# A tuned decoder layer whose opening takes sixteen column chunks instead of twelve, in four block groups instead of five

## The chip, the cores and the metric

One core of a Trainium2 chip runs the whole layer. The metric is the device time of one execution in microseconds, the median of several runs. Of the five engines this text speaks of PE (TensorE: matrix products), DVE (VectorE), ACT (ScalarE) and SP (SyncE, which here only issues DMAs, strictly in the order in which the program lists them).

## The reference

A decoder layer on 256 tokens of width 2048, all in float32. The part that the change touches is the first feed-forward block with its modulation:

```python
c_act = jax.nn.silu(c)
mod = (c_act @ w_ada[l] + b_ada[l]).reshape(b, N_MOD, D_MODEL)       # 9 vectors of 2048
h = modulate(rms_norm(x, norm_ffn1[l]), mod[:, 0], mod[:, 1])        # h * (1 + scale) + shift
x = x + 0.5 * mod[:, 2][:, None, :] * swiglu(h, w_ffn1_gu[l], w_ffn1_down[l])
...
gate, up = jnp.split(h @ w_gu, 2, axis=-1)                           # each 5632 wide
return (jax.nn.silu(gate) * up) @ w_down
```

After it come a retention and a window-attention mixer with their projections, a second feed-forward block and a last norm.

## The kernel before

**Products.** A float32 product is made of three products of rounded halves. A weight block is 128 x 512. ACT rounds it to its high part (`wh`, L350), DVE subtracts to get the low part (`wl`, L352), and PE multiplies, for each of the two halves of the 256 tokens, high by high, low activation by high weight, and high by low weight (L342, L343, L344): six products of 512 columns a block. Blocks are mostly handled in pairs (one ACT cast, one DVE subtraction of 128 x 1024, twelve products). `wsp` holds three such pairs, so casts and subtractions run at most a little ahead of PE. Weights come by DMA into `raw`, four buffers of 1 MB.

**Conditioning.** Each of the nine vectors of `mod` has 16 parts of 128 values, and each part needs one row block of `w_ada` (1 MB, called a row here), multiplied and summed on DVE by `ada_pass` (L206): two passes of 1024 columns a row in the opening, four of 512 later.

**The opening.** The activation `h` needs shift and scale (vectors 0 and 1), that is 32 rows, before all of it is there. So that PE need not wait for all of them, the contraction over 16 blocks is cut into groups (`bounds`), and `group(ks)` makes the rows and then the columns `h` of the next group while PE multiplies those of the present one. In each group PE visits all column chunks in turn (512 columns of the gate or the up half; an even and an odd chunk make a pair that gives 512 columns of the result). `visit` loads the chunk's blocks of that group into `raw` and multiplies; the sums are kept in `part` between groups (`to_parts`: copied by ACT the first time, L984, added by DVE later, L982). `stay` leaves the last two chunks of a group in PSUM, since the next group visits the chunks in the opposite order and starts with them. In the last group `swiglu_up` adds both parts (L665, L666), applies silu on ACT and multiplies (L669), and the result is turned by four PE transposes a tile (L477). A ring of two rows (`ring`, the halves of `tiles[0]`) holds the rows of the opening.

Before the change there are twelve chunks (`EARLY = 6` pairs) and groups of 2, 3, 3, 4 and 4 blocks. Pairs 6 to 10 are then made by `ffn_up`, whole contraction at once; pairs 6 to 9 are turned by DMA transposes (`turn_by_dma`: two ACT copies, a transpose issued by SP, two ACT copies), pair 10 by PE.

**Later rows.** The next three vectors (48 rows) are made by `conditioning`, a generator paced by `tick`: each half of a weight load of `ffn_up` and of the down projection advances it by `rate` quarter rows. It starts after the opening, at 192 quarter rows for 150 halves, from a ring of two rows in a slot of its own.

**What sets the order.** SP follows the program. The order on PE, DVE and ACT is made by a scheduler when the program is built; on the chip each engine follows that order and waits where an operand is not there.

Of the kernel before, what the change touches and what calls it, by code (L numbers as in the profile page):

```python
# [9 lines left out]
F32 = mybir.dt.float32  # L10
# [7 lines left out]
P = 128  # L18
# [3 lines left out]
NT = S // P  # L22
# [3 lines left out]
KB = 4  # L26
EPS = 1e-6
RAWS = 4
EARLY = 6

RH, RDK, RDV = 8, 128, 256
QH, KVH, HD = 32, 8, 64
# [45 lines left out]
def layer_kernel(  # L78
# [40 lines left out]
    def nm(s):  # L119
        uid[0] += 1  # L120
        return f"{s}_{uid[0]}"
# [110 lines left out]
    def two_rows():  # L232

        both = slot()
        turn = [both[:, :D], both[:, D:]]

        def place():
            turn.append(turn.pop(0))
            return turn[-1]

        return place

    def conditioning(outputs, place, ahead, behind):


        tiles = [(m, k) for m, _, _ in outputs for k in range(KD)]
        held = {}
        step = 0
        for m, gain, row in outputs:
            sums = ada_sums()  # L250
            for k in range(KD):
                for q in range(AQ):
                    for i in range(step // AQ, min((step + ahead) // AQ + 1, len(tiles))):
                        if i not in held:
                            held[i] = place()
                            ada_load(*tiles[i], held[i])
                    if behind is not None and step < 2 * AQ:
                        with tc.issue_after(behind.ins):
                            ada_pass(k, held[step // AQ], sums, q)
                    else:  # L260
                        ada_pass(k, held[step // AQ], sums, q)
                    step += 1
                    if k == KD - 1 and q == AQ - 1:
                        ada_end(m, slice(0, KD), sums, gain)
                        if row is not None:
                            gate_out(m, row)
                    yield
# [19 lines left out]

    def set_pace(outputs, halves, place, ahead):
        assert next(pace["steps"], None) is None
        pace["steps"] = conditioning(outputs, place, ahead, pace["behind"])  # L290
        pace["rate"] = len(outputs) * KD * AQ / halves
        pace["due"] = 0.0

    def tick():
        pace["due"] += pace["rate"]
        while pace["due"] >= 1.0:
            pace["due"] -= 1.0
            next(pace["steps"], None)
# [47 lines left out]
    def split(pool, tag, src, n, hi_engine="act"):  # L346
        k = src.shape[1]
        hi = pool.tile([P, 2, n], F32R, tag=tag + "h", name=nm(tag + "h"))[:, :k, :]
        lo = pool.tile([P, 2, n], F32R, tag=tag + "l", name=nm(tag + "l"))[:, :k, :]
        cast.append(nc.scalar.copy(hi, src).ins)  # L350
        del cast[:-1]
        nc.vector.tensor_sub(lo, src, hi.bitcast(F32))  # L352
        return hi, lo
# [3 lines left out]
    def pair_tile():  # L357
        return asp.tile([P, 2, CH], F32, tag="a", name=nm("a"))
# [525 lines left out]
    tiles = [slot(), part[0]]  # L884
    ring = [tiles[0][:, :D], tiles[0][:, D:]]

    def part_of(n):
        at = (n % 4) * NT * CH
        return [part[n // 4][:, at + t * CH : at + (t + 1) * CH] for t in range(NT)]

    early = [ada_sums() for _ in range(2)]

# [21 lines left out]
    def group(ks):  # L914

        for k in ks:
            for m in (1, 0):
                if (m, k) not in rows_of:
                    place(m, k)
                for q in range(passes):  # L920
                    ada_pass(k, rows_of[m, k], early[m], q, passes)
                if ks[0] == 0:
                    ada_end(m, slice(k, k + 1), early[m], 0 if m else None, passes)
                yield
        if ks[0] > 0:
            for m in (1, 0):
                ada_end(m, slice(ks[0], ks[-1] + 1), early[m], 0 if m else None, passes)
        for k in ks:
            ps = bank()
            for t in range(NT):  # L930
                xn = t512()[:, :P]
                nc.scalar.mul(xn, x_sb[:, t, k * P : (k + 1) * P], r[t])
                nc.tensor.transpose(ps[:, t * P : (t + 1) * P], xn, ident)
            modulated(held, k, ps[:, :S], 0, act=True)
# [7 lines left out]
    r = [Root(ssq, t).all() for t in range(NT)]  # L942
    for t in range(NT):
        nc.vector.tensor_scalar(out=r[t], in0=r[t], scalar1=HALF, scalar2=None, op0=ALU.mult)
    bounds = (0, 2, 5, 8, 12, 16)
    groups = [range(a, b) for a, b in zip(bounds, bounds[1:])]


# [3 lines left out]
    def load_blocks(n, ks):  # L952
        raw = raws.tile([P, KB, CH], F32, tag="raw", name=nm("raw"))
        c0 = (n % 2) * DFF + (n // 2) * CH
        nc.sync.dma_start(
            raw[:, : len(ks), :],
            gu[ks[0] * P : (ks[-1] + 1) * P, c0 : c0 + CH].rearrange("(k p) n -> p k n", p=P),
        )
        return raw

    def visit(n, ks, raw, ends, step=2):
        starts = n not in banks
        if starts:
            banks[n] = [acc_bank() for _ in range(NT)]
        for a in range(0, len(ks), step):
            b = min(a + step, len(ks))
            hl = slice(ks[a], ks[a] + b - a)
            wh, wl = split(wsp, "w", raw[:, a:b, :], CH)
            products(
                banks[n],  # L970
                held.hi[:, hl, :],
                held.lo[:, hl, :],
                wh,
                wl,
                starts and a == 0,
                b == len(ks) and ends,
            )

    def to_parts(n):
        for p, b in zip(part_of(n), banks.pop(n)):  # L980
# [3 lines left out]
                nc.scalar.copy(p, b)  # L984
        moved.add(n)

    for _ in group(groups[0]):
        pass
    for g, ks in enumerate(groups):
        final = g == len(groups) - 1  # L990
        order = chunks if g % 2 == 0 else chunks[::-1]
        coming = iter(()) if final else group(groups[g + 1])
        due = 0 if final else 2 * len(groups[g + 1])
        stay = () if final else order[-2:]
        for i, n in enumerate(order):
            visit(n, ks, load_blocks(n, ks), n not in stay)
            last = len(order) - 2
            for _ in range((i + 1) * due // last - i * due // last if i < last else i == last):
                next(coming, None)
            if n in stay:  # L1000
                continue
            if not final:
                to_parts(n)
            elif n % 2:
                swiglu_up(
                    banks.pop(n - 1), banks.pop(n), tiles, n // 2, (part_of(n - 1), part_of(n))
                )
    gate = gate_row()
    tiles.append(slot())
    place = two_rows()  # L1010
    set_pace([(2, None, 0.5), (4, 1, None), (3, None, None)], 150, place, AQ)
    ffn_up(held, gu, tiles, EARLY, turned=range(EARLY, DFF // CH - 1))
    gate_in = gate_load(gate, 2)
    wi = w_in[0]
# [395 lines left out]
```

## Time and profile before

| | |
|---|---|
| runs shown | 2403.92, 2406.2, 2407.77 us; median 2406.2 |
| the profiled execution | 2404.94 us, of which 2403.2 us are the span from its first to its last instruction |
| PE busy | 2369.4 us, 99% of the span |
| DVE, ACT busy | 1693.1 us (70%), 1300.2 us (54%) |
| HBM read | 595.06 MB, 248 GB/s over the span |

A product's record shows its latency, so records of PE overlap: how fast PE works is read from the distance between the starts of products that follow each other, and lost time from the idle rows and from distances that are longer.

### The profile page before, as it was taken

To read this page: it belongs to the slowest core of one execution; us is meant where nothing else is said; L and a number is where in the kernel's file an instruction comes from. 1 tells how busy PE (TensorE), PEld (TensorE's weight loads), DVE (VectorE), ACT (ScalarE), POOL (GpSimd) and SP (SyncE) were. 2 spreads that over 40 slices of the span, in tenths; PEclk is the share of its full clock that TensorE was granted. 3 is DMA by queue.
4 is the path that set the end of the run, shared out by engine and by line. 5 is a ranking of instruction groups with operands and counts; after the bars stand their busy time and mean duration, and the time that the engine had idled before them with its cause. 6 is when DMAs were issued, how large, how long until landed. Compare 5 with 4: busy or idle time off the path is not lost. (4 is left out here: it accounts for less than half of the span.)

```text
span 2403.2 us, 28875 instructions
## 1 busy us (share of the span) xinstructions
PE 2369.4 (99%) x10662; PEld 1936.5 (81%) x10662; DVE 1693.1 (70%) x2720; ACT 1300.2 (54%) x1811; POOL 5.6 (0%) x14
## 2 busy tenths in 40 slices
PE   7999999999999999999999999999999999999998
PEld 4778888888788887778888888887888888888886
DVE  6998787778877667886766766768655555545656
ACT  6544545454546566765555554456445445454544
POOL 0000000000000000000000000000000000000000
PEclk9999999999999999999999999999999999999999
DMA  9987688998876797766679787765677777765563
GB/s 347 338 334 285 230 308 301 379 320 304 302 269 228 243 286 219 232 229 210 217 256 289 263 282 264 280 198 200 225 239 237 248 256 240 261 219 189 183 205 126
DMA packets 309550, 615.31 MB, mean 256 GB/s; under 512 B 75105, under 2 KB 75489, under 8 KB 290593
## 3 DMA queue, kind: packets, MB, share of 16 engines
q1 hardware_dynamic: 307906, 606.82, 74.1%
q0 software_dynamic: 928, 5.61, 0.6%
q8 instruction: 83, 1.36, 0.2%
q10 hardware_dynamic: 576, 1.05, 0.1%
q14 instruction: 57, 0.47, 0.1%
HBM read 595.06 MB, written 2.12 MB: 248 GB/s over the span
## 5 line engine op out<-in xcount | busy, mean ns | idle before, releaser
L352 DVE TENSOR_TENSOR wl<-raw,wh 128x1024 fp32r<-128x1024 f32 (+1 forms) x806 | 967.9, 1206 | 559.4 <-ACT wh L350 554.6
L350 ACT CAST wh<-raw 128x1024 fp32r<-128x1024 f32 (+1 forms) x806 | 836.9, 1041 | 938.6 <-PE pa L343 921.7
L342 PE MATMUL pa<-wh,hh 128*128 128x512 f32 x2192 | 857.1, 392 | 2.2 <-ACT wh L350 1.7
L343 PE MATMUL pa<-wh,hl 128*128 128x512 f32 x2192 | 856.2, 391 | 1.6 <-DVE hl L599 1.6
L344 PE MATMUL pa<-wl,hh 128*128 128x512 f32 x2192 | 784.2, 392 | 2.4 <-DVE wl L352 2.2
L342 PEld LDWEIGHTS pa<-wh,hh 128*128 128x128 f32 x2192 | 412.0, 188 | 90.1 <-issue 2.8
L343 PEld LDWEIGHTS pa<-wh,hl 128*128 128x128 f32 x2192 | 412.1, 188 | 89.7 <-issue 3.0
L344 PEld LDWEIGHTS pa<-wl,hh 128*128 128x128 f32 x2192 | 409.4, 188 | 92.9 <-DVE wl L352 6.8
L343 PE MATMUL pa<-wh,a 128*128 128x512 f32 x944 | 365.3, 389 | 0.1
L342 PE MATMUL pa<-wh,a 128*128 128x512 f32 x944 | 349.8, 390 | 1.0 <-ACT wh L350 0.5
L344 PE MATMUL pa<-wl,a 128*128 128x512 f32 x944 | 349.0, 390 | 1.4 <-DVE wl L352 1.4
L344 PEld LDWEIGHTS pa<-wl,a 128*128 128x128 f32 x944 | 176.9, 188 | 39.9 <-DVE wl L352 3.2
L342 PEld LDWEIGHTS pa<-wh,a 128*128 128x128 f32 x944 | 177.1, 188 | 39.7 <-DVE slot L1292 1.0
L343 PEld LDWEIGHTS pa<-wh,a 128*128 128x128 f32 x944 | 177.1, 188 | 37.2 <-DVE a L385 0.5
L206 DVE CUSTOM_DVE_ANT_0 slot<-slot,cact 128x512 f32<-128x512 f32 (+1 forms) x252 | 192.6, 812 | 14.4 <-DMA slot<-in_w_ada_dram 14.3
L206 DVE CUSTOM_DVE_ANT_0 raw<-raw,cact 128x512 f32<-128x512 f32 (+1 forms) x260 | 167.0, 695 | 46.0 <-DMA raw<-in_w_ada_dram 39.1
L510 ACT COPY slot<-back 128x512 uint16<-128x512 uint16 x124 | 82.7, 766 | 0.0
L385 DVE TENSOR_TENSOR a<-slot,a 128x512 fp32r<-128x512 f32 x118 | 80.6, 683 | 1.7 <-ACT a L384 1.7
L384 ACT CAST a<-slot 128x512 fp32r<-128x512 f32 x118 | 72.7, 617 | 0.0
L494 ACT COPY flat<-t 128x512 uint16<-128x512 uint16 x112 | 63.5, 616 | 9.6 <-DVE t L1197 9.2
L206 DVE DVE_READ_ACCUMULATOR2_ANT sums<- 128x1 f32 x512 | 41.8, 82 | 0.0
L982 DVE TENSOR_TENSOR slot<-slot,pa 128x512 f32<-128x512 f32 x56 | 35.7, 677 | 0.0
(197 smaller groups left out, 1163.9 us busy)
## 6 DMA issues: line engine op xcount, KB each, us to landing
raw<-in_w_ffn_gu_dram SPq DMA_DIRECT2D x152, 1024.0 KB, 5.2
raw<-in_w_in_dram SPq DMA_DIRECT2D x104, 1024.0 KB, 5.4
raw<-in_w_ffn_down_dram SPq DMA_DIRECT2D x88, 1024.0 KB, 5.1
slot<-in_w_ada_dram SPq DMA_DIRECT2D x76, 1024.0 KB, 7.4
raw<-in_w_ada_dram SPq DMA_DIRECT2D x64, 1024.0 KB, 5.0
raw<-in_w_ffn_gu_dram SPq DMA_DIRECT2D x24, 768.0 KB, 6.9
raw<-in_w_swa_branch_dram SPq DMA_DIRECT2D x16, 1024.0 KB, 5.1
raw<-in_w_ret_branch_dram SPq DMA_DIRECT2D x16, 1024.0 KB, 5.3
```

The lines of the kernel that those rows point to most:

```text
L206: nc.vector.tensor_tensor_reduce(out=w[:, at], in0=w[:, at], in1=cact[:, at], scale=1.0, scalar=0.0, op0=ALU.mult, op1=ALU.add, accum_out= ...
L342: nc.tensor.matmul(ps, ah[:, j, ts], wh[:, j, :], start=first, stop=False)
L343: nc.tensor.matmul(ps, al[:, j, ts], wh[:, j, :], start=False, stop=False)
L344: nc.tensor.matmul(ps, ah[:, j, ts], wl[:, j, :], start=False, stop=last)
L350: cast.append(nc.scalar.copy(hi, src).ins)
L352: nc.vector.tensor_sub(lo, src, hi.bitcast(F32))
L384: nc.scalar.copy(hi, v)
L385: nc.vector.tensor_sub(lo, v, hi.bitcast(F32))
L494: nc.scalar.copy(planes[:, i, :], words(src)[:, :, i])
L510: nc.scalar.copy(into[:, :, :, i], held["turned"][:, i])
L982: nc.vector.tensor_add(p, p, b)
```

## The change

`EARLY` becomes 8, so the opening takes 16 column chunks, and `bounds` becomes (0, 2, 6, 12, 16): groups of 2, 4, 6 and 4. `visit` now loads its blocks itself, in pieces of at most four blocks: a visit of the group of six takes two `raw` buffers. The sums of chunks 0 and 1 are kept in four tiles of the `back` pool, those of 14 and 15 in two `pair_tile`s, since `part` holds twelve. The visiting order is such that the last group runs forward. Beside the last group eight of the later 48 rows are made (one quarter row a pair of blocks); these take their place in `raw`, among the weights, until the slot of the two-row ring is free. The remaining 160 quarter rows follow at 160 to 117 halves. Of the eight pairs of the opening, pairs 1 and 5 are turned by DMA, the other six by PE; pairs 6 and 7, turned by DMA before, are now turned by PE.

```diff
-EARLY = 6
+EARLY = 8
...
-    def conditioning(outputs, place, ahead, behind):
+    def conditioning(outputs, place, behind):
...
-                    for i in range(step // AQ, min((step + ahead) // AQ + 1, len(tiles))):
+                    for i in range(step // AQ, min((step + pace["ahead"]) // AQ + 1, len(tiles))):
...
+    beside = [pair_tile() for _ in range(2)]
+    behind = [[back.tile([P, CH], F32, tag="back", name=nm("back")) for _ in range(NT)] for _ in range(2)]
...
     def part_of(n):
-        at = (n % 4) * NT * CH
-        return [part[n // 4][:, at + t * CH : at + (t + 1) * CH] for t in range(NT)]
+        if n < 2:
+            return behind[n]
+        if n >= 14:
+            return [beside[n - 14][:, t, :] for t in range(NT)]
+        at = ((n - 2) % 4) * NT * CH
+        return [part[(n - 2) // 4][:, at + t * CH : at + (t + 1) * CH] for t in range(NT)]
...
-    bounds = (0, 2, 5, 8, 12, 16)
+    bounds = (0, 2, 6, 12, 16)
...
-    def visit(n, ks, raw, ends, step=2):
+    def visit(n, ks, ends, ticks=False):
...
+        raw_of = [(load_blocks(n, part), part) for part in (ks[:KB], ks[KB:]) if part]
+        pieces = [
+            (raw[:, a : a + 2, :], part[a : a + 2])
+            for raw, part in raw_of
+            for a in range(0, len(part), 2)
+        ]
...
+            if ticks:
+                tick()
...
+    ROWS_FFN1 = [(2, None, 0.5), (4, 1, None), (3, None, None)]
+    row_ring = []
+
+    def place_row():
+        return row_ring[0]() if row_ring else raw_row()
...
-        order = chunks if g % 2 == 0 else chunks[::-1]
+        if final:
+            set_pace(ROWS_FFN1, 32 * 192 // 32, place_row, 1)
+        order = chunks if (len(groups) - g) % 2 else chunks[::-1]
...
-            visit(n, ks, load_blocks(n, ks), n not in stay)
+            visit(n, ks, n not in stay, final)
+            if final:
+                turn_step()
...
-                    banks.pop(n - 1), banks.pop(n), tiles, n // 2, (part_of(n - 1), part_of(n))
+                    banks.pop(n - 1),
+                    banks.pop(n),
+                    tiles,
+                    n // 2,
+                    (part_of(n - 1), part_of(n)),
+                    n // 2 in (1, 5),
...
-    place = two_rows()
-    set_pace([(2, None, 0.5), (4, 1, None), (3, None, None)], 150, place, AQ)
+    row_ring.append(two_rows())
+    pace["rate"] = (192 - 32) / 117
+    pace["ahead"] = AQ
```

The first place where the order differs is DVE in the third group. Before (groups of three blocks), two visits stand there: `wl` is a weight's low part, `slot_129` with `cact` a row's pass, `slot_127` with `pa` the addition of a kept sum.

```order
L352 TENSOR_TENSOR wl_1226<-raw_1221,wh_1225 128x1024
L206 ISA slot_129,sums_131<-slot_129,cact 128x1024
L206 ISA sums_131 128x1
L206 ISA slot_129,sums_131<-slot_129,cact 128x1024
L206 ISA sums_131 128x1
L352 TENSOR_TENSOR wl_1242<-raw_1221,wh_1241 128x512
L982 TENSOR_TENSOR slot_127<-slot_127,pa_1188 128x512
L982 TENSOR_TENSOR slot_127<-slot_127,pa_1189 128x512
L352 TENSOR_TENSOR wl_1261<-raw_1256,wh_1260 128x1024
```

After, the third group has six blocks a visit, and the same names read:

```order
L998 TENSOR_TENSOR slot_127<-slot_127,pa_1713 128x512
L998 TENSOR_TENSOR slot_127<-slot_127,pa_1714 128x512
L206 ISA slot_129,sums_137<-slot_129,cact 128x1024
L206 ISA sums_137 128x1
L206 ISA slot_129,sums_137<-slot_129,cact 128x1024
L206 ISA sums_137 128x1
L353 TENSOR_TENSOR wl_1811<-raw_1776,wh_1810 128x1024
L353 TENSOR_TENSOR wl_1835<-raw_1830,wh_1834 128x1024
L353 TENSOR_TENSOR wl_1851<-raw_1830,wh_1850 128x1024
L998 TENSOR_TENSOR slot_127<-slot_127,pa_1772 128x512
```

Between one chunk's two additions and the next chunk's there are now three full subtractions where there were one and a half.

The second place is SP in the last group. Before, there are only weight loads (L955), until the opening ends and the first row of the ring follows:

```order
L955 DMA raw_2364<-in_w_ffn_gu_dram 128x4x512
L955 DMA raw_2422<-in_w_ffn_gu_dram 128x4x512
L955 DMA raw_2458<-in_w_ffn_gu_dram 128x4x512
L327 DMA raw_2521<-in_w_ffn_gu_dram 128x4x512
L201 DMA slot_2518<-in_w_ada_dram 128x2048 x2
```

After, a row (L201, into a `raw` buffer) follows every second weight load (L963):

```order
L963 DMA raw_2434<-in_w_ffn_gu_dram 128x4x512
L963 DMA raw_2472<-in_w_ffn_gu_dram 128x4x512
L201 DMA raw_2507<-in_w_ada_dram 128x2048
L963 DMA raw_2522<-in_w_ffn_gu_dram 128x4x512
L963 DMA raw_2560<-in_w_ffn_gu_dram 128x4x512
L201 DMA raw_2595<-in_w_ada_dram 128x2048
```

The third place is DVE at the row `raw_2507` of that list. Its four passes stand between the two subtractions of one weight load, where before (L352) nothing but additions (L666) and products (L669) of the finished pair stood:

```order
L352 TENSOR_TENSOR wl_2255<-raw_2234,wh_2254 128x1024
L666 TENSOR_TENSOR slot_127<-pa_2178,slot_127 128x512
L666 TENSOR_TENSOR slot_127<-pa_2179,slot_127 128x512
L669 TENSOR_TENSOR t_2212<-t_2212,slot_127 128x512
L352 TENSOR_TENSOR wl_2275<-raw_2270,wh_2274 128x1024
```

After:

```order
L353 TENSOR_TENSOR wl_2437<-raw_2434,wh_2436 128x1024
L206 ISA raw_2507,sums_2351<-raw_2507,cact 128x512
L206 ISA sums_2351 128x1
L206 ISA raw_2507,sums_2351<-raw_2507,cact 128x512
L206 ISA sums_2351 128x1
L206 ISA raw_2507,sums_2351<-raw_2507,cact 128x512
L206 ISA sums_2351 128x1
L206 ISA raw_2507,sums_2351<-raw_2507,cact 128x512
L206 ISA sums_2351 128x1
L353 TENSOR_TENSOR wl_2454<-raw_2434,wh_2453 128x1024
```

The weight `wl_2454` behind the four passes is thus queued behind the landing of the row.

More of the change, by code (lines that the diff above doesn't have):

```diff
@@ L289, in set_pace @@
         assert next(pace["steps"], None) is None
-        pace["steps"] = conditioning(outputs, place, ahead, pace["behind"])
+        pace["steps"] = conditioning(outputs, place, pace["behind"])
         pace["rate"] = len(outputs) * KD * AQ / halves
         pace["due"] = 0.0
+        pace["ahead"] = ahead
     def tick():
@@ L964, in visit @@
             banks[n] = [acc_bank() for _ in range(NT)]
[L965 to L968, printed above, removed]
+        raw_of = [(load_blocks(n, part), part) for part in (ks[:KB], ks[KB:]) if part]
[4 more added lines that the diff above has]
+        ]
+        for raw, part in pieces:
+            a, b = part[0] - ks[0], part[-1] + 1 - ks[0]
+            hl = slice(part[0], part[-1] + 1)
+            wh, wl = split(wsp, "w", raw[:, : len(part), :], CH)
             products(
```

## The prediction

> **What bounds the kernel now.** I read the page's engine shares first, then a table of stretches, then what PE waited for, then DVE's own order.
>
> ```profile
> PE 2369.4 (99%) x10662; PEld 1936.5 (81%) x10662; DVE 1693.1 (70%) x2720; ACT 1300.2 (54%) x1811; POOL 5.6 (0%) x14
> ```
>
> PE is busy for 99% of the span, so only its idle time and its slow stretches can be won. The table of stretches shows where they lie. Its columns are the stretch in us, its length, busy time and records of PE, PEld, DVE, ACT and POOL, granted clock, DMA share, GB/s. The bounds are the starts of the first product of each block group (counted off: 144, 216, 216, 288 and 288 products).
>
> ```profile
> 0.00:25.96 25.96, 9.83 (x15) 3.76 (x15) 13.19 (x47) 13.67 (x32) 0.20 (x4) 1.00 0.87 319
> 25.96:64.10 38.14, 37.13 (x148) 29.23 (x149) 31.46 (x46) 27.30 (x46) 0.00 (x0) 1.00 0.97 369
> 64.10:114.23 50.13, 49.94 (x224) 40.90 (x222) 45.68 (x72) 25.04 (x37) 0.00 (x0) 1.00 0.89 334
> 114.23:171.30 57.07, 52.95 (x226) 40.09 (x225) 54.11 (x88) 25.88 (x41) 0.00 (x0) 1.00 0.88 326
> 171.30:238.04 66.74, 66.74 (x300) 54.82 (x299) 60.22 (x85) 32.12 (x45) 0.00 (x0) 1.00 0.82 304
> 238.04:308.18 70.14, 70.14 (x331) 58.26 (x330) 56.23 (x83) 39.82 (x51) 0.00 (x0) 1.00 0.65 230
> 308.18:720.00 411.82, 410.58 (x1813) 337.93 (x1812) 324.09 (x575) 203.97 (x241) 2.23 (x4) 1.00 0.88 314
> 720.00:2403.20 1683.20, 1672.04 (x7617) 1371.48 (x7615) 1108.16 (x1730) 932.42 (x1324) 3.17 (x6) 1.00 0.70 233
> ```
>
> PE idles 16.1 us before the first product, which the change does not touch: the first group still has two blocks and the same first loads. Of the rest of the opening, the third group stands out: PE idles 4.1 us in it and DVE is busy for 54.11 of 57.07 us. PE's waits up to 500 us name the releaser (total, times, longest):
>
> ```profile
> ...
> PE pa L344 <- DVE wl L352: 2.2, 5, 0.8
> PE pa L342 <- ACT wh L350: 1.7, 2, 0.9
> PE pa L343 <- DVE hl L599: 1.6, 2, 1.2
> PE pa L342 <- DVE slot L982: 0.5, 1, 0.5
> ```
>
> All but the ACT row are DVE being late.
>
> **Prices.** From PE's timeline (start, duration): two of the first products, a pair of transposes, and two products with 50 others between them. Below them the group of PE's transposes of results (count, busy us, mean ns).
>
> ```profile
> 29.12 0.63 PE L342 MATMUL pa<-wh,hh 128*128 128x512 f32 x1
> 29.55 0.63 PE L343 MATMUL pa<-wh,hl 128*128 128x512 f32 x1
> ...
> 118.04 0.38 PE L933 MATMUL ps<-small_c,t 128*128 128x128 f32 x2
> ...
> 128.06 0.39 PE L342 MATMUL pa<-wh,hh 128*128 128x512 f32 x1
> ...
> 139.66 0.39 PE L343 MATMUL pa<-wh,hl 128*128 128x512 f32 x1
> ```
>
> ```profile
> L477 PE MATMUL ps<-small_c,t 128*128 128x128 f32 x32 | 4.5, 272 | 0.0
> ```
>
> A product costs (139.66 - 128.06)/51 = 0.2275 us, so a pair of blocks 2.73. One transpose's record is 0.27 long and that of two 0.38, so the second starts 0.11 after the first: 0.11 each. The first products stand 0.43 apart although the granted clock reads 1.00; that slow start, some 2.9 us in all until 32 us, stays.
>
> DVE's starts in a stretch without idle time:
>
> ```profile
> 94.92 1.22 DVE L352 TENSOR_TENSOR wl<-raw,wh 128x1024 fp32r<-128x1024 f32 x1
> 96.05 1.21 DVE L206 CUSTOM_DVE_ANT_0 slot<-slot,cact 128x1024 f32<-128x1024 f32 x1
> ...
> 97.20 1.22 DVE L206 CUSTOM_DVE_ANT_0 slot<-slot,cact 128x1024 f32<-128x1024 f32 x1
> ...
> 98.34 0.68 DVE L352 TENSOR_TENSOR wl<-raw,wh 128x512 fp32r<-128x512 f32 x1
> 98.95 1.27 DVE L982 TENSOR_TENSOR slot<-slot,pa 128x512 f32<-128x512 f32 x2
> 100.14 1.22 DVE L352 TENSOR_TENSOR wl<-raw,wh 128x1024 fp32r<-128x1024 f32 x1
> ...
> 115.62 0.42 DVE L599 TENSOR_TENSOR hl<-t,hh 128x256 fp32r<-128x256 f32 x1
> ...
> 293.48 0.69 DVE L206 CUSTOM_DVE_ANT_0 slot<-slot,cact 128x512 f32<-128x512 f32 x1
> ...
> 294.10 0.68 DVE L206 CUSTOM_DVE_ANT_0 slot<-slot,cact 128x512 f32<-128x512 f32 x1
> ```
>
> From start to start: a subtraction of a pair 1.14, of one block 0.61; a row of two passes 2.29; an addition 0.60; a column of `h` 0.42 at most; a pass of 512 0.61.
>
> **The group sizes.** DVE's work against PE's, group by group. Before, third group: 12 visits of 1.75 for subtractions is 21.0, 8 rows 18.3, 20 additions 12.0, 4 columns 1.7: 53.0 us, against 216 products and 8 transposes, 50.0 us. DVE is overloaded by 6%, and the stage takes 57.07. The second comes to 45.7 of 49.8, the fourth to 59.4 of 66.4. After, the same sums:
> - first group: 16 x 1.14 + 8 x 2.29 + 4 x 0.42 = 38.2 us of DVE against 192 products, 43.7 us (87%; before 28.7 of 32.8, also 87%);
> - second: 32 x 1.14 + 12 x 2.29 + 24 x 0.60 + 6 x 0.42 = 80.9 against 384 products and 12 transposes, 88.7 (91%);
> - third: 48 x 1.14 + 8 x 2.29 + 28 x 0.60 + 4 x 0.42 = 91.5 against 576 products, 131.9 with transposes (69%);
> - last: 32 x 1.14 + 32 passes at 0.61 + 48 additions and multiplications = 84.8 against 384 products and 48 transposes, 92.6 (92%; before 53.9 of 70.8).
>
> So no group overloads DVE any more, because the same 32 rows are spread over a third more products. What DMA must bring falls too. For the old third group it is 36 blocks (0.262 MB) and 8 rows (1.049 MB), 17.8 MB in 49.1 us of products, 363 GB/s; the new third needs 256, the second 336, the last 272. The first group needs 16.8 MB in 43.7 us, 384 GB/s, and before it was 12.6 MB in 32.8, the same.
>
> **What PE loses after.** Before, from 25.96 to 308.18 PE took 282.2 us for 1152 products (262.1), 28 transposes of `h` (3.1) and 48 of results (5.3): 11.7 lost, of which about 7.1 in the third group, 2.9 in the slow start and 1.8 elsewhere in the first; the other stages come out at nothing in sum. After I charge: the slow start 2.9; the first group 1.9, since most of its 1.8 is one wait on ACT at its end (0.9 us, with some slow restarts), and I take that to come once a group, not once a visit; the second group 0.4, as its DVE share is that of the old second and fourth, which lost 0.3 each; the third 0.2; the last 0.6. Sum 6.0, so 5.7 us are won. A bound on each: nothing lost beyond the slow start would win 8.8; the old third group's loss once more in the new second would make it a loss of 1.0.
>
> In the first group a rule weighs against the change. The last row here has DMA's highest sustained rate in the opening:
>
> ```profile
> 60.00:80.00 20.00, 20.00 (x92) 16.43 (x91) 16.15 (x24) 13.28 (x25) 0.00 (x0) 1.00 1.02 388
> ```
>
> At the first stage's 369 GB/s the new first group is 1.8 us short of PE's pace, the old one 1.3; the four loads in flight cover that. The Trainium skill, "DMA: Bandwidth & Descriptors", section Specifications, gives about 358 GB/s as the limit of HBM for one core: by it the new group would be 3.2 us short, the old 2.3, and I would take 0.4 us off the gain. The 388 above goes past that figure, so I leave the sum as it is.
>
> **The eight rows beside the last group.** A row now sits in `raw`, and DVE's order puts its four passes between two subtractions, which wait behind it. The trace has such rows in later stages. The first line is DVE's waits for them between 850 and 1500 us, the second a stretch of that stage, the last the page's DMA issues (count, size, median us to landing):
>
> ```profile
> ...
> DVE raw L206 <- DMA raw<-in_w_ada_dram: 29.6, 23, 3.2
> ...
> ```
>
> ```profile
> 1000.00:1500.00 500.00, 499.31 (x2317) 408.07 (x2316) 353.02 (x658) 285.25 (x434) 0.00 (x0) 1.00 0.74 248
> ```
>
> ```profile
> ...
> slot<-in_w_ada_dram SPq DMA_DIRECT2D x76, 1024.0 KB, 7.4
> raw<-in_w_ada_dram SPq DMA_DIRECT2D x64, 1024.0 KB, 5.0
> ```
>
> Each wait is 1.3 us, and PE lost 0.7 us in 500 there. But DVE is 71% busy there, not 92%. Eight rows at 1.3 us make 10.4 us of waiting; DVE's slack in the last group is 92.6 - 84.8 = 7.8, and it runs up to one pair, 2.7 us, ahead: 10.5. So the waits just fit, and 0.6 us is what I charge; with none 0, with 3.2 us each 25.6 - 10.5 = 15.1. In the order three subtractions, each paced by PE at 2.73, mostly lie between the freeing of a row's buffer and its first pass, 8.2 us against a landing of 5.0 to 7.4: nearer to the low end.
>
> **The rest.** Pairs 1 and 5 go to DMA and 6 and 7 come from it: 16 PE transposes fewer and 16 more, zero. Their ACT copies lie beside an ACT that is 57% busy in the last group (39.82 of 70.14). SP passes four transposes in the last group; their planes are copied by ACT a visit earlier, so the loads behind them do not wait. After the opening 160 quarter rows come at 1.37 a half, not 1.28: 0.09 x 0.61 = 0.05 us of DVE on 2.73. The fullest stretch there leaves room:
>
> ```profile
> 660.00:680.00 20.00, 20.00 (x90) 16.53 (x90) 17.84 (x35) 9.66 (x12) 0.00 (x0) 1.00 0.97 352
> ```
>
> 17.84 would become 18.2 of 20: nothing, or at worst the 1.2 us that PE now idles from 308 to 720 once more. Everything after 720 keeps its order.
>
> **Sum.** The profiled execution took 2404.94 us, 1.3 below the median of 2406.2. Less 5.7 it is 2399.2; against the median, 2400.5.
>
> **Rivals.** First, the waits come back at the group borders. In the old third group four waits (1.15, 0.42, 0.52, 0.40 us by the waits, 3.2 with the restarts) came in its first 13 us, when `h` was late because a row's pass had waited for DMA:
>
> ```profile
> 109.78 0.68 DVE L352 TENSOR_TENSOR wl<-raw,wh 128x512 fp32r<-128x512 f32 x1
> 112.19 1.23 DVE L206 CUSTOM_DVE_ANT_0 slot<-slot,cact 128x1024 f32<-128x1024 f32 x1 [1.72 <-DMA slot<-in_w_ada_dram]
> ```
>
> The other borders cost next to nothing. One such border leaves a gain of 2.5 (2403.7), two a small loss of 0.7 (2406.9). For it: two borders of the new order, at 91% and 87% of DVE. Against: in the new order the rows ahead of them have longer leads.
>
> Second, and slower: the rows in `raw` hold up DVE in the last group. At 3.2 us each PE loses 15.1 there instead of 0.6: 2400.5 + 14.5 = 2415.0. It decides the sign from waits of about 2.1 us a row (16.8 - 10.5 = 6.3 lost, which eats the gain).
>
> Third, the later stage does not take 1.37 quarter rows a half: 152 halves with 192 quarter rows become 120 with 160, and if DVE's 0.05 us a half were not hidden at all PE would lose 120 x 0.05 = 6 us, 2406.5. Against it stands the free tenth of DVE above.
>
> **Chances.** About 0.2%, 4.8 us, is what a measurement of this kernel can tell from no change. My forecast gets 0.68, of which 0.62 lie over that bound (the sum is 0.9 above it, its best case 4.0) and 0.06 under it. The first rival gets 0.16 and the third 0.03, all within the bound; the second 0.13, slower. That is faster 0.62, same 0.25, slower 0.13. The range reaches from 8.8 won on the profiled execution (2396.1, and half a us for the spread of runs) to two bad borders at 2406.9; outside it lies the second rival.
>
> **What would show it.** The last products of the four groups should end near 75, 164, 296 and 389 us, the last against 308.2 plus 384 products, 395.6, for the same work before. DVE should be busy for 65 to 75% of the third group, and `PE pa L344 <- DVE wl` should nearly vanish from the waits before 300. If PE idles over 3 us in the last group behind a subtraction whose predecessor on DVE is a row's pass that waited for DMA, the second rival holds; if it idles at about 75 or 164 behind `hl`, the first.

## The result, and the profile after

The changed kernel takes 2401.06 us (median of 13 runs, 2398.03 to 2402.71), the kernel before 2404.52 beside it (13 runs, 2403.4 to 2411.71): a ratio of 0.998, 95% interval 0.9971 to 0.9988. That is 0.1 to 0.3% faster, 3.5 us between the medians. The profiled execution took 2398.28 us, its span 2396.5.

The page's engine shares hardly differ from before:

```profile
PE 2365.2 (99%) x10662; PEld 1937.3 (81%) x10662; DVE 1696.6 (71%) x2707; ACT 1302.2 (54%) x1807; POOL 5.6 (0%) x14
```

The stretches of the changed kernel, cut at the first product of each of its four groups (192, 384, 576 and 384 products), with the columns as in the prediction:

```profile
24.77:74.36 49.59, 47.40 (x196) 37.43 (x197) 41.44 (x58) 35.81 (x58) 0.00 (x0) 1.00 0.99 376
74.36:162.50 88.14, 88.14 (x394) 72.68 (x392) 80.70 (x113) 40.56 (x50) 0.00 (x0) 1.00 0.92 340
162.50:296.48 133.98, 133.44 (x593) 109.36 (x592) 100.53 (x132) 61.62 (x82) 0.00 (x0) 1.00 0.75 260
296.48:388.16 91.68, 91.68 (x426) 76.15 (x425) 86.42 (x151) 55.50 (x72) 0.00 (x0) 1.00 0.88 299
388.16:720.00 331.84, 330.07 (x1462) 272.39 (x1461) 270.99 (x486) 167.34 (x200) 2.23 (x4) 1.00 0.90 318
```

The group that lost most is gone. In the old third group DVE was busy for 54.11 us beside 50.0 of PE's own work. Now it is busy for less than PE's work in every group: for 100.53 of 133.98 us in the large third one (75%), and for 86.42 of 91.68 in the last (94%), which loses nothing all the same. PE's waits up to 600 us (total, times, longest) show what is left:

```profile
...
PE pa L343 <- ACT wh L351: 2.9, 4, 0.9
...
PE pa L344 <- DVE hl L600: 0.3, 1, 0.3
PE pa L345 <- DVE wl L353: 0.2, 1, 0.2
```

DVE's rows have shrunk from 4.3 to 0.5 us; the wait on ACT has grown from 1.7 to 2.9, of which in both 0.8 is the wait of the very first product. What DVE waited for in the last group, with the eight rows among the weights:

```profile
...
DVE raw L206 <- DMA raw<-in_w_ada_dram: 2.0, 3, 1.0
```

**Where the time came from.** Each row of this table is a profiled execution: the start of the first product, then the time from it to product 1536 (the opening's work, done by both structures), and three lengths behind it, counted in products. All are differences of starts in PE's timeline.

| profile | first product | to 1536 | 1536 to 2112 | to 2640 | to 3168 | sum of the four |
|---|---|---|---|---|---|---|
| before | 25.96 | 370.20 | 130.72 | 121.93 | 122.82 | 745.67 |
| changed | 24.77 | 363.39 | 131.67 | 120.60 | 123.72 | 739.38 |
| changed, `again` | 26.35 | 363.63 | 131.68 | 120.59 | 123.58 | 739.48 |
| changed, `again2` | 26.79 | 363.85 | 131.67 | 120.60 | 125.28 | 741.40 |

The opening wins 6.4 to 6.8 us. One of them returns at once, because eight of PE's transposes now lie behind product 1536 and not ahead of it. A second part returns at products 2640 to 3168, 0.8 us in two profiles and 2.5 in the third. The start of the first product differs by 2.0 us between three profiles of the same program. These are the two places at which the three profiles differ. The 2.5 us contain a stretch of 3.41 us at half the granted clock (last section). One such stretch lowers the mean clock of a run by 0.0007 (half of 3.41 in 2400 us). Of the thirteen runs the seven with a mean granted clock of 0.998 took 2400.99 to 2402.71 us, the six with 0.999 took 2398.03 to 2401.06. That this stretch is why the median gain is 3.5 us and not 6 fits these figures, but no run isolates it.

### The profile page after: what moved, and what is told of

The parts are those of the page before. It is cut to its first block, busy times and chain, and to the rows that moved or that the text cites. A ratio compares the mean times of both kernels' runs of the same rounds, so it can differ in the third digit from the quotient of the medians.

```text
span 2396.5 us, 28841 instructions
## 1 busy us (share of the span) xinstructions
PE 2365.2 (99%) x10662; PEld 1937.3 (81%) x10662; DVE 1696.6 (71%) x2707; ACT 1302.2 (54%) x1807; POOL 5.6 (0%) x14
## 5 line engine op out<-in xcount | busy, mean ns | idle before, releaser
L353 DVE TENSOR_TENSOR wl<-raw,wh 128x1024 fp32r<-128x1024 f32 x794 | 967.2, 1224 | 553.0 <-ACT wh L351 548.8
L351 ACT CAST wh<-raw 128x1024 fp32r<-128x1024 f32 x794 | 835.1, 1053 | 932.3 <-PE pa L344 903.2
L206 DVE CUSTOM_DVE_ANT_0 raw<-raw,cact 128x512 f32<-128x512 f32 (+1 forms) x296 | 189.9, 696 | 46.8 <-DMA raw<-in_w_ada_dram 40.0
L206 DVE CUSTOM_DVE_ANT_0 slot<-slot,cact 128x512 f32<-128x512 f32 (+1 forms) x216 | 170.2, 838 | 8.6 <-DMA slot<-in_w_ada_dram 8.6
```

Of the source, the lines that this page charges most:

```text
L206: nc.vector.tensor_tensor_reduce(out=w[:, at], in0=w[:, at], in1=cact[:, at], scale=1.0, scalar=0.0, op0=ALU.mult, op1=ALU.add, accum_out= ...
```

## The experiments

Two theories stood against each other. The first: DVE had more work than PE in the old third group, and larger groups over more chunks take that away. The second: that group lost its time to DMA. Beside them stood the eight rows and the way in which pairs are turned. The changed kernel ran again on the chip of the first experiments:

> The changed kernel itself once more. Its thirteen runs fall into two clusters, near 2398.4 and near 2401.4 us, and the profile came from the lower one. Theory A (the won time is DVE's overload of the old third group, and does not vary) expects the four group stages as in the first profile, 49.6, 88.1, 134.0 and 91.7 us, and any difference of some 3 us outside them, at the start or after 720 us. A rival (a wait at a group border comes or goes with the landing of a row) expects one stage to be about 3 us longer in a slow run.

2399.96 us (11 runs, 2398.19 to 2405.41), ratio 0.9979 (0.997 to 0.9988). The four stages took 49.8, 88.1, 134.1 and 91.6 us in its profile, and 49.9, 88.1, 134.2 and 91.6 in that of `again2` (a later repeat, below), which is 2.6 us longer: the difference lies outside the four stages, as the first theory said, at the first product and near 650 us.

**The kernel before, with half of DVE's work on the rows, and with half of their DMA.** The first edit does one of a row's two passes in the groups after the first:

```diff
-                for q in range(passes):
+                for q in range(passes if ks[0] == 0 else 1):
...
-                ada_end(m, slice(ks[0], ks[-1] + 1), early[m], 0 if m else None, passes)
+                ada_end(m, slice(ks[0], ks[-1] + 1), early[m], 0 if m else None, 1)
```

> The kernel before, with only the first of a row's two passes done in the groups after the first; the second half of those sums is left out. Loads are unchanged: DVE's work on rows is halved (24 x 1.14 = 27 us less in 244 us), DMA's is the same. My theory, DVE's overload: the old third group loses 7.1 us of PE time because DVE has 53.0 us of work against 50.0; with 43.9 it should lose under 2. Rival, DMA: the group needs 363 GB/s and gets 326, and rows land late; then its loss stays at 5 or more.

The second loads half a row and lets both passes read it:

```diff
-    def ada_pass(k, w, sums, q, passes=AQ):
+    def ada_pass(k, w, sums, q, passes=AQ, again=False):
...
-            in0=w[:, at],
+            in0=w[:, : D // passes] if again else w[:, at],
...
-        ada_load(m, k, rows_of[m, k], 2 if k < 2 else 1)
+        if k < 2:
+            ada_load(m, k, rows_of[m, k], 2)
+        else:
+            nc.sync.dma_start(
+                rows_of[m, k][:, : D // 2],
+                w_ada[(m * KD + k) * P : (m * KD + k + 1) * P, : D // 2],
+            )
...
-                    ada_pass(k, rows_of[m, k], early[m], q, passes)
+                    ada_pass(k, rows_of[m, k], early[m], q, passes, k >= 2)
```

> The kernel before, with the rows after the first two of each set loaded only in their first half; both passes read that half, so DVE's work is unchanged and the sums are not those of the reference. What the old third group must bring falls from 17.8 MB to 13.6 MB (277 GB/s against 363). My theory, DVE's overload: 53.0 us of DVE against 50.0 stays, so at least 4 of the 7.1 us lost in the third group stay; the part that began with a row landing late may go. Rival, DMA: the loss falls under 2.

They took 2398.64 and 2403.38 us, one run each. The old third group (216 products) in the table of stretches, first with half of DVE's work on the rows:

```profile
113.39:163.14 49.75, 49.75 (x222) 40.85 (x221) 42.88 (x67) 24.36 (x37) 0.00 (x0) 1.00 0.98 356
```

Then with half of the rows' DMA:

```profile
110.32:165.88 55.56, 52.58 (x224) 41.86 (x222) 52.86 (x85) 23.63 (x34) 0.00 (x0) 0.97 0.78 263
```

With half of DVE's work on the rows the group takes 49.75 us instead of 57.07 and loses 0.2, although DMA brings more a second than before (356 GB/s against 326). With half of the rows' DMA, at 263 GB/s, it takes 55.56 us and loses 5.8. PE's waits there are all on DVE; the last line is DVE's own wait for rows:

```profile
PE pa L342 <- DVE slot L988: 1.8, 1, 1.8
PE pa L344 <- DVE wl L352: 1.2, 2, 0.9
...
DVE slot L206 <- DMA slot<-in_w_ada_dram: 2.3, 2, 1.2
```

That settles it for this group: DVE's work was the bound, and not the rate of DMA. The 1.5 us by which its loss of 7.3 fell in the second run are not the late landings that the prediction named: DVE waited 2.3 us for rows there, 1.4 before, and 1.0 of the 2.3 lies ahead of the stop of 1.8. PE's idle time fell from 4.1 to 3.0 us, and about 1.7 of the 5.8 us are slow products at half the granted clock behind that stop (last section).

**The changed kernel with the old five groups.**

```diff
-    bounds = (0, 2, 6, 12, 16)
+    bounds = (0, 2, 5, 8, 12, 16)
```

> The changed kernel with the old groups of 2, 3, 3, 4, 4 blocks on its sixteen chunks. Theory A (DVE): in the third group 16 visits cost DVE 28.0 for subtractions, 18.3 for rows, 16.8 for additions, 1.7 for columns, 64.8 us against 66.4 of PE, 98%; that stage loses 1 to 3 us, the whole is 1 to 3 us above the changed kernel. Rival B (DMA was the limit of the old third group, at 363 GB/s): 21.0 MB in 65.5 us is 320 GB/s, no loss there, the whole as the changed kernel.

2402.24 us (11 runs), ratio to before 0.9991 (0.9982 to 1.0); `again` on the same chip 2399.96. The third group of three blocks, over sixteen chunks:

```profile
140.08:209.28 69.20, 67.39 (x294) 53.83 (x292) 64.43 (x100) 30.09 (x41) 0.00 (x0) 1.00 0.88 321
```

It loses 3.2 us, where twelve chunks lost 7.3 and the new groups lose 1.2 in theirs. DVE is busy for 64.43 us against 66.4 of PE's work, 97%, and PE's waits name `wl`:

```profile
PE pa L345 <- DVE wl L353: 1.5, 3, 0.8
...
```

All of the change but the group sizes brings 2.6 us, the group sizes 2.3 more. Not all of the latter lies in the opening, which takes 364.72 us to product 1536 with the old groups and 363.39 to 363.85 with the new ones, 0.9 to 1.3 us less. Products 2640 to 3168 take 125.43 us here, a length in which the changed kernel's own profiles differ by 1.7. So most of the opening's gain comes with the sixteen chunks and the rest of the change, and about 1 us of it with the group sizes. They win 2.0 us in the third group and give some away in the first: with the old sizes it had no stop on ACT and lost 2.7 us, the slow start alone, where the changed kernel loses 5.5.

**The kernel before with the new groups and twelve chunks.** `visit` and the visiting order as in the change, and

```diff
-    bounds = (0, 2, 5, 8, 12, 16)
+    bounds = (0, 2, 6, 12, 16)
```

> The kernel before, twelve chunks, with the new groups of 2, 4, 6, 4 and nothing else of the change. Theory A (DVE): second group 67.0 us of DVE against 66.8 of PE, 100%, loses about 2 us; third 73.0 of 99.2, loses nothing; the whole wins about 5 us on the kernel before. Rival B (DMA): the second group needs 25.2 MB in 65.5 us of products, 384 GB/s, more than the old third group's 363, so it loses 6 us or more and the whole wins nothing.

2417.08 us (5 runs), ratio 1.0051 (1.0039 to 1.0064): 12 us slower, where the first theory had been read as a gain. The first three groups:

```profile
25.93:70.49 44.56, 37.51 (x148) 27.73 (x149) 36.81 (x53) 27.73 (x45) 0.00 (x0) 1.00 0.96 360
70.49:148.87 78.38, 71.86 (x297) 56.01 (x296) 67.50 (x99) 31.76 (x45) 0.00 (x0) 0.96 0.88 335
148.87:249.54 100.67, 100.39 (x449) 82.26 (x448) 77.41 (x102) 48.54 (x67) 0.00 (x0) 1.00 0.76 272
```

The third group loses only 0.6 us, but the first and second lose 11.4 and 12.0. A second group of four blocks pulls eight rows into twelve visits of the first. With the prediction's prices DVE then has 12 x 1.14 + 8 x 2.29 + 4 x 0.42 = 33.7 us of work against 32.8 of products, and in the second group 24 x 1.14 + 12 x 2.29 + 20 x 0.60 + 6 x 0.42 = 69.4 against 66.8. DMA would have to bring 14.7 MB in 32.8 us, 448 GB/s, and brought 360; in the second group 384, and brought 335. By these sums both engines are overloaded. The expected gain came from a sum of the first theory that was 2.4 us too low for the second group (67.0) and not made for the first; the rival's 6 us or more for the second group was nearer. PE's waits between 30 and 150 us, and ACT's longest in the second group:

```profile
PE pa L342 <- ACT wh L350: 10.3, 7, 2.4
PE pa L344 <- DVE wl L352: 2.4, 6, 0.7
...
ACT wh L350 <- DMA raw<-in_w_ffn_gu_dram: 27.5, 6, 8.1
...
```

The trace leans to DMA: PE waited mostly for ACT's casts and ACT for weights to land, while DVE was busy for only 83 and 86% of the two groups. But SP's queue stood for 37.7 us of the second group behind the sums that free a row's buffer, so DVE's part in the late loads is not excluded, and which engine came first stays open.

So the larger groups need the sixteen chunks, which give each visit order a third more products to lay rows beside. The sixteen chunks with the rest of the change gain 2.6 us without them in the run above, with an interval that just reaches no gain.

**The changed kernel without the eight rows beside the last group.** All 192 quarter rows come after the opening, at 192 to 117 halves:

```diff
-            set_pace(ROWS_FFN1, 32 * 192 // 32, place_row, 1)
+            pass
...
-            visit(n, ks, n not in stay, final)
+            visit(n, ks, n not in stay)
...
-    pace["rate"] = (192 - 32) / 117
-    pace["ahead"] = AQ
+    set_pace(ROWS_FFN1, 117, place_row, AQ)
```

> The changed kernel without the eight later rows beside the last group; all 192 quarter rows come after the opening, at 192 for 117 halves (1.64 instead of 1.37). Theory A with the prediction's term for the rows (0.6 us charged in the last group, nothing after it): the last group is 0 to 0.6 us shorter; afterwards DVE needs 1.14 + 1.64 x 0.61 + 0.34 = 2.48 us of 2.73 a half and the weights and rows 0.95 MB, 350 GB/s, so PE loses 1 to 5 us between 388 and 720 us. If the rows beside the last group were what hurts, this kernel would be faster than the changed one.

2405.52 us (11 runs), ratio 1.0003 (0.9994 to 1.0012): the whole gain is gone. The opening takes 363.29 us to product 1536 instead of 363.39, with 36 transposes of results ahead of that product instead of 40 (0.44 us), so no cost of the eight rows can be read there. It is the next stage that loses: 133.33, 125.35 and 122.39 us in the three lengths of the table above, 5.1 more than the changed kernel. From PE's timeline there, the largest stop:

```profile
555.57 0.61 PE L343 MATMUL pa<-wh,a 128*128 128x512 f32 x2
558.25 0.50 PE L344 MATMUL pa<-wh,a 128*128 128x512 f32 x1 [2.06 <-DVE a L386]
...
559.62 0.63 PE L343 MATMUL pa<-wh,a 128*128 128x512 f32 x1
560.04 0.63 PE L344 MATMUL pa<-wh,a 128*128 128x512 f32 x1
560.47 0.63 PE L345 MATMUL pa<-wl,a 128*128 128x512 f32 x1
560.90 0.63 PE L343 MATMUL pa<-wh,a 128*128 128x512 f32 x1
```

DVE was at the four passes of a row when `a` was wanted. PE stood for 2.06 us, and the products behind the stop start 0.43 apart, not 0.2275, until 562.

**All pairs turned by PE, or four by transfers.**

```diff
-                    n // 2 in (1, 5),
+                    False,
```

> The changed kernel with all eight pairs of the opening turned by PE and none by transfers. PE has 16 transposes more at 0.11 us: 1.8 us more than the changed kernel, 2401.5 to 2403, if the transfers were free there. Rival: the transfers of pairs 1 and 5 cost as much in held-up loads as they save on PE; then there is no difference.

2405.04 us (11 runs), ratio 1.0 (0.9991 to 1.0009): 3.5 to 5 us slower than the changed kernel's three medians, where 1.8 was the most that either theory gave. The last group, up to the start of its last product, takes 93.27 us instead of 91.4, the 16 transposes at 0.11. The rest is one place in the later stage, 127.63 us in the table's last length instead of 123.7. From DVE's timeline at that place:

```profile
656.56 1.22 DVE L353 TENSOR_TENSOR wl<-raw,wh 128x1024 fp32r<-128x1024 f32 x1
659.11 0.69 DVE L206 CUSTOM_DVE_ANT_0 slot<-slot,cact 128x512 f32<-128x512 f32 x1 [1.33 <-DMA slot<-in_w_ada_dram]
...
661.56 1.22 DVE L353 TENSOR_TENSOR wl<-raw,wh 128x1024 fp32r<-128x1024 f32 x1
```

And PE's waits from 388 to 780 us:

```profile
PE pa L345 <- DVE wl L353: 2.5, 2, 2.1
...
```

A row landed 1.33 us late, the subtraction behind its passes was late, and PE stopped for 2.1 us and again ran at 0.43 a product behind it. Why the row is late there, with four transfers fewer on SP, I have not shown.

```diff
-                    n // 2 in (1, 5),
+                    n // 2 in (1, 3, 5, 7),
```

> The changed kernel with four of the opening's eight pairs turned by transfers (1, 3, 5 and 7) and not two. PE has 16 transposes fewer at 0.11 us: if the transfers are free, 1.8 us less than the changed kernel, 2398 to 2399 us. Rival: SP's queue holds the loads behind the four transposes of a pair for a landing, and the last group (92% of DVE) or the next stage loses 1 us or more a pair; then it is no faster than the changed kernel, or up to 3 us slower.

2398.76 us (10 runs), ratio 0.9976 (0.9967 to 0.9985), on the chip of the run before. Repeated beside the changed kernel:

> The kernel with four turned pairs once more, beside the changed kernel on the same chip. By PE's 16 transposes at 0.11 us it is 1.8 us below the changed kernel; the rival, transfers that hold up loads, sees no difference.

> The changed kernel once more, for the comparison with the two above on one chip: 2399.5 to 2401.5 us, 4 to 5 us below the kernel before.

2398.99 (9 runs; 2398.78 without one of 4703.32), 0.9976 (0.9966 to 0.9986), against 2401.53 (11 runs), 0.9985 (0.9976 to 0.9994). In the profiles the last group is 0.9 us shorter and the next length too (130.72 instead of 131.67), the 16 transposes; the transfers are free there. But behind product 3168 both profiles of this kernel are some 3 us longer than those of the changed kernel. The place is the same in both; in the first profile it reads:

```profile
1434.07 0.69 DVE L206 CUSTOM_DVE_ANT_0 raw<-raw,cact 128x512 f32<-128x512 f32 x1 [5.30 <-DMA raw<-in_w_ada_dram]
...
1437.80 0.74 PE L345 MATMUL pa<-wl,hh 128*128 128x512 f32 x2 [2.10 <-DVE wl L353]
```

A row landed 5.3 us late (2.5 in `again2`, where PE does not stop), PE stopped for 2.1 us, and the products behind it start 0.43 apart. Whether the transfers, 1000 us earlier, bring this about is not shown. The 2.5 us between the medians are measured; that they are the 16 transposes alone is not.

**ACT's order in the first group.** In the changed kernel ACT does this at the first of two stops:

```profile
45.45 0.59 ACT L1000 COPY slot<-pa 128x512 f32<-128x512 f32 x1 [1.45 <-PE pa L345]
45.94 1.05 ACT L351 CAST wh<-raw 128x1024 fp32r<-128x1024 f32 x1
46.88 0.59 ACT L1000 COPY slot<-pa 128x512 f32<-128x512 f32 x1
```

The copy of a finished sum waits 1.45 us for PE, and the cast that PE needs next stands behind it. The edit, on top of four turned pairs, puts a chunk's copies behind the next chunk's cast:

```diff
+    kept = []
...
             if n in stay:
+                if kept:
+                    with tc.issue_after(cast[-1]):
+                        to_parts(kept.pop(0))
                 continue
-            if not final:
+            if g == 0:
+                kept.append(n)
+                if len(kept) > 1:
+                    with tc.issue_after(cast[-1]):
+                        to_parts(kept.pop(0))
+            elif not final:
                 to_parts(n)
```

> The kernel with four turned pairs, in which ACT's two copies of a chunk's sums in the first group are put behind the cast of the next chunk. In the three profiles of the changed opening with this group ACT had a copy ahead of that cast twice, the copy waited for PE, and PE then waited 0.94 and 0.93 us for the cast. Theory: the stop is a matter of ACT's order; both stops go, and with the wait of 0.20 beside them 2.0 us are won against four turned pairs. Rival: the cast was late for its buffer or its load and not for the copy ahead of it; then PE waits there as long for ACT or for DMA, and the time does not move.

2397.38 us (7 runs), ratio 0.9969 (0.9959 to 0.998): the fastest of all, 4.2 us below the changed kernel on the same chip and 1.6 below four turned pairs, with an interval that overlaps that one's. The first group is 1.6 us shorter than in `four_turned2`. PE's waits in it:

```profile
PE pa L345 <- DVE wl L353: 0.9, 1, 0.9
PE pa L343 <- ACT wh L351: 0.8, 1, 0.8
```

The two stops on ACT at 46 and 67 us are gone, and in place of the second DVE is late once, by 0.9. The 0.8 on ACT left over is the wait of the group's first product, which is there in the changed kernel too.

## Why the prediction was right, and where not

- **DVE's overload of the old third group, the main step, holds.** Halving DVE's work on the rows took 7.1 of the 7.3 us, halving their DMA 1.5. The new groups have DVE at 84, 92, 75 and 94% of their length, predicted 87, 91, 69 and 92% of PE's work, and the subtraction's waits are down to 0.2 us. The third is fuller than predicted in part because four more columns and six passes of the later rows lie in it. (The 272 GB/s given for the last group is taken over 92.6 us; over its products alone, as for the other groups, it is 288. Measured were 299.)
- **The ends of the groups** were to be near 75, 164, 296 and 389 us; they came at 74.4, 162.5, 296.5 and 388.2, from a first product 1.2 us earlier than in the profile of before; in the two other profiles they came 1.8 to 2.5 us later.
- **What PE still loses** was to be 6.0 us and is 6.5, with the shares wrong. The first group loses 5.5 where 2.9 + 1.9 stood. The slow start took 1.9; it is 1.5 to 2.9 in the thirteen profiles, by no edit. The wait on ACT came twice and not once, and cost 3.6 with what follows it: that it comes once a group was the step that failed. Putting ACT's copies behind the casts took it away; the number of visits alone does not bring it, since the same sixteen visits with the old groups had none. The third loses 1.2 instead of 0.2, at its border, where `hl` is late: the first rival at about a third of its price. The second and the last lose nothing (0.4 and 0.6 charged).
- **The rows in `raw`** were to wait 8 x 1.3 us and waited 2.0 in all, in three of eight; the 1.3 us read from the later stage were too high a price. The second rival needed 2.1 us for each.
- **The later stage** was charged at nothing, and this is the term that was mis-sized. Products 2112 to 2640 win 1.3 us, products 2640 to 3168 lose 0.8 in two profiles and 2.5 in the third. The prediction saw the fullest stretch, took its free tenth as cover, and charged at worst the 1.2 us idle there once more. What loses there is PE waiting for a gated addition (L606) that DVE has queued behind the four passes of a row. The prediction did not price a stop that slow products follow: one such place costs 3.9 us in `no_rows` and 4.0 in `pe_turned`. The third rival's place was right, its mechanism (0.05 us a half) was not.
- **What the eight rows are for** was not priced at all. Without them the gain of the opening, some 5 us, is spent again in the next stage.
- **The transposes at zero** hold for the change (16 fewer, 16 more), but not their neighbourhood: two pairs more by transfers measure 2.5 us less and two fewer 3.5 to 5 us more, where the transposes' own time is 1.8.
- **The sum.** 2400.5 was predicted, 2401.06 measured. The prediction's 11.7 us of loss before the change count 48 transposes of results ahead of product 1152, where 40 lie; with 40 it is 12.6, and these 0.9 are what returns behind product 1536. The opening's gain, 6.4 to 6.8 us less the 1.0 of transposes that return, is 5.4 to 5.9 against 5.7. In `again2`, whose time is nearest to its median, the later stage takes back 1.1 of it and a late first product 0.8, which leaves 3.4. That the forecast came out so near all the same is luck in part: it started from the median of three runs, 2406.2, and thirteen runs of the kernel before gave 2404.52.

## What to carry to other kernels

Sum each engine's work by stage and not over the kernel, for the new sizes as well as for the old: a stage at 106% loses its time, the same work at 75 to 94% does not, and the same sum would have told that the new groups with twelve chunks overload the first two, though not that they would lose 11 and 12 us. When work is moved out of a full stage, look at the stage that receives it or is next to it, since a little more work there can turn a covered wait into a stop of PE (1.64 quarter rows a half instead of 1.37 did it in `no_rows`). An engine's order can make a stop that no resource makes: if the waiting instruction stands behind one that itself waits for PE, reordering two instructions is enough.

## What the runs showed of the hardware

A stop of PE can cost nearly twice its length, because the granted clock falls to half behind it. Behind a stop of 2.06 us (`no_rows`) the next products lost another 1.7 us, and behind 2.11 us (`pe_turned`) also 1.7; behind 1.79 us with a second stop of 0.34 close by (half of the rows' DMA) it was 2.0; behind single stops of 0.8 to 0.95 us it was 0.1 to 0.5. The rows of `no_rows` and `pe_turned`, cut to the slow products, show the granted clock at 0.50:

```profile
558.78:562.19 3.41, 3.41 (x10) 2.62 (x9) 3.41 (x9) 0.20 (x1) 0.00 (x0) 0.50 1.06 397
...
663.87:667.28 3.41, 3.41 (x10) 2.63 (x9) 1.48 (x2) 1.56 (x2) 0.00 (x0) 0.50 0.43 103
```

The same program goes either way. In the profile of the changed kernel, three short stops where DVE gates the first results of the block (L606):

```profile
644.67 0.50 PE L343 MATMUL pa<-wh,a 128*128 128x512 f32 x1 [0.91 <-DVE t L606]
645.01 0.40 PE L344 MATMUL pa<-wh,a 128*128 128x512 f32 x1
645.87 0.51 PE L343 MATMUL pa<-wh,a 128*128 128x512 f32 x1 [0.47 <-DVE t L606]
...
647.00 0.73 PE L345 MATMUL pa<-wl,a 128*128 128x512 f32 x2 [0.40 <-DVE wl L353]
647.58 0.39 PE L343 MATMUL pa<-wh,a 128*128 128x512 f32 x1
647.80 0.40 PE L344 MATMUL pa<-wh,a 128*128 128x512 f32 x1
```

The same place in the profile of `again2`, the same kernel:

```profile
647.40 0.50 PE L343 MATMUL pa<-wh,a 128*128 128x512 f32 x1 [1.16 <-DVE t L606]
...
649.73 1.22 PE L345 MATMUL pa<-wl,a 128*128 128x512 f32 x2 [0.34 <-DVE wl L353]
650.75 0.63 PE L343 MATMUL pa<-wh,a 128*128 128x512 f32 x1
651.17 0.63 PE L344 MATMUL pa<-wh,a 128*128 128x512 f32 x1
651.60 0.63 PE L345 MATMUL pa<-wl,a 128*128 128x512 f32 x1
```

The rows of the two places, the first whole and the second cut to the slow products:

```profile
644.00:655.00 11.00, 9.47 (x39) 7.25 (x40) 11.00 (x20) 6.38 (x14) 0.00 (x0) 1.00 0.88 323
...
649.14:652.55 3.41, 3.07 (x8) 2.24 (x8) 3.41 (x6) 0.00 (x0) 0.00 (x0) 0.50 0.47 182
```

With a first stop of 0.91 us the products go on at 0.23, with 1.16 they go on at 0.43 for 2.5 us, and the length to product 3168 is 125.28 us instead of 123.72. The length of the longest stop does not settle it. At this place the kernel with the old groups fell to half clock behind stops of 1.09, 0.47 and 0.40 us, while those with four turned pairs kept the full clock behind 1.21 and 0.40; and a stop of 2.39 us in the kernel with twelve chunks and the new groups cost only 0.5 more.

The Trainium skill, "TensorE: Matmul & The Clock Gate", Part 1 on the HAM clock gate, gives 426.7 ns between products of 512 columns at half clock, and a gate whose window of about 3.4 us runs free. The traces agree with 0.43 us between products and with 3.41 us at 0.50 in each of the three slow rows above, and a window that runs free would make the same program go either way as here. It puts the fall to half clock after an idle window of about 3.4 us; here stops of 1.1 us (with two shorter ones behind it) to 2.1 us were enough. So the slow products are shown to be the granted clock, and how much idle time brings it down stays open. A clock of 0.95, which the profile of `no_rows` shows almost throughout, does not slow the products: its second group takes 88.14 us as in the changed kernel.

The slow first products are not seen in the rows. In the profile of the kernel before, the first record of the granted clock begins at 31.98 us, where these slow products end, and the 1.00 that the prediction read ahead of it stands for a stretch without a record.

The start of the first product, which no edit touches, lies between 24.6 and 26.8 us in the thirteen profiles. That alone is a spread of 2.2 us, about as much as most of these differences: single executions cannot tell them apart, medians of ten or so runs or lengths counted from the first product can.
